# Stick-breaking attention: two heads' values become one 128-column stationary, their transposed weights move as 256 columns in three fp32r products, and the buffer pools change from 17 and 5 to 16 and 7

## The chip, the core and the metric

The kernel runs on one core of one Trainium2 chip, as one program. The metric is device time in microseconds (us), from the runs listed below. The engines are named as the profile names them: PE is the matmul engine and PEld its weight loads, DVE the vector engine, ACT the scalar engine, POOL the engine that starts gathers and scatters, SP the queue that starts the weight loads from HBM.

## The reference

The program is a two-layer trunk over 512 tokens of width 1024. Layer 0 mixes tokens with a state-space mixer and a pooling mixer. Layer 1 mixes them with stick-breaking attention. Each layer then has a mixture of 16 experts. Only the attention is touched by the change:

```python
# 16 heads x 64, strictly causal, swept in 128-query blocks
for blk in range(s // SB_BLOCK):
    q0 = blk * SB_BLOCK
    end = q0 + SB_BLOCK
    z = jnp.einsum('bhqd,bhkd->bhqk', q[:, :, q0:end], k[:, :, :end]) * scale
    causal = s_pos[None, :] < t_pos[:, None]
    log_keep = jnp.where(causal, jax.nn.log_sigmoid(-z), 0.0)
    log_after = lax.cumsum(log_keep, axis=3, reverse=True) - log_keep
    wts = jnp.where(causal, jnp.exp(jax.nn.log_sigmoid(z) + log_after), 0.0)
    outs.append(jnp.einsum('bhqk,bhkd->bhqd', wts, v[:, :, :end]))
```

## The kernel before

**Products.** Most products are in float32 split in two parts: `split` (L81 to L83) writes a high part with ACT and a low part (source minus high) with DVE, both of type fp32r. `mm3` (L85 to L89) then makes three products: stationary high with moving high (L87), stationary high with moving low (L88), stationary low with moving high (L89). A few products are made in plain float32. In the trace each plain float32 matmul stands as two records and each fp32r matmul as one.

**Attention.** `mixer1` (L615 to L717) projects values (`vproj`, 96 products), queries (`query`) and keys (`key`, 48 products each) and runs eight calls of `attend(g, o)`, each for two heads. The program's order is v0, q0, k0, A00, q1, A01, k1, A10, v1, q2, A11, k2, A20, q3, A21, k3, A30, A31, out projection; A20 is `attend(2, 0)`. An attend runs over four query blocks `qb`, with n = 128, 256, 384 and 512 keys. For both heads `s` of a block: scores into a bank of tag B (L672 to L674), two sigmoids on ACT (L676, L677), a running product on DVE (the scan, L679), a product on DVE (L680); then 128x128 transposes into a bank of tag T (L686), a copy back to SBUF (L687, on ACT or DVE, whichever the planner finds free), and the products with the values (L691) in plain float32. In L691 the two heads have 64 stationary columns each, and write to the two halves of one bank `po`, which is kept for the whole attend and split into the output `cat` at its end (L693). L664 writes one element of `po` at the start of the attend.

**Buffers.** Slots of tag raw hold 8 KB for each partition (`NR` = 17 of them): the streamed weights, and every large tile (inputs, transposed inputs, values, queries, keys, outputs). Buffers of tag h hold 4 KB (`NH` = 5). PSUM has four banks of tag A (projections, `po`, the out projection, which needs all four at once, L728), two of B and two of T.

**What sets the order.** The kernel is written in the program's order above, and a planner in the framework puts each engine's instructions in an order of their own: of the instructions that are ready it takes the earliest of the program. So a projection fills PE while an attend that stands before it in the program waits for ACT and DVE. Buffers of one tag are handed out in the order in which the program first writes them: a bank of tag A cannot be taken by a projection before the `po` that stands ahead of it in the program has been written once. Each engine then works through its own list in order, and waits for the others by semaphores. `weights` (L109) splits a streamed weight into a ring of buffers (tags wh, wl) and first asks for the loads that lie one (attention) or six (experts) ahead.

The lines that the prediction's steps touch:

```python
            po = self.bank("A", "pA")            # L663
            v.memset(po[:, 0:1], 0.0)            # L664
...
                kw = [self.half4("kw"), self.half4("kw")]          # L668
...
                    nc.any.tensor_copy(kp[:, :n], pT[:, :n])       # L687
...
            self.split(cat[hh][:, pg * 2 + o], cat[2 + hh][:, pg * 2 + o], po)   # L693
...
        ps = [self.bank("A", "pA") for _ in range(NT)]             # L728
```

Of the kernel before, what the change touches and what calls it, by code (L numbers as in the profile page):

```python
# [8 lines left out]
F32R = mybir.dt.float32r  # L9
BF = mybir.dt.bfloat16  # L10
I32 = mybir.dt.int32
AF = mybir.ActivationFunctionType
# [5 lines left out]
NT = 4  # L18
# [2 lines left out]
EPS = 1e-5  # L21
NE = 16
CAP = 96
NR = 17
RING = 6
NH = 5
GATES = (-1, -1, 7, 15)
OVER = 12
NEG = -1e30
# [9 lines left out]
class Trunk:  # L39
# [18 lines left out]
    def slot(self, name, dt=F32):  # L58
        return self.sb.tile([128, 2048], dt, tag="raw", bufs=NR, name=name)

    def half4(self, name, dt=F32):
        return self.sb.tile([128, 1024], dt, tag="h", bufs=NH, name=name)

# [551 lines left out]
    def mixer1(self):  # L615
        nc, v = self.nc, self.nc.vector
        X = self.xt_pair("x2T")
        for i in range(NT):
            self.transposes(self.xt[i], i, X)
        cat = [None] * 4  # L620
        st = [{}, {}]

        def vproj(hh):
            w = self.weights(1) + self.weights(1)
            vs = self.slot(f"v{hh}").rearrange("p (i d) -> p i d", i=NT)
            for i in range(NT):
                p = self.bank("A", "pA")
                self.proj_x(p, i, X, w)
                nc.scalar.activation(vs[:, i], p, AF.Copy)
            return vs  # L630

        def heads():
            w = self.weights(1)
            for o in range(2):
                p = self.bank("A", "pA")
                for kb in range(KB):
                    os = slice(o * 128, (o + 1) * 128)
                    self.mm3(p, (w[kb][0][:, os], w[kb][1][:, os]), self.op(X, kb), kb == 0, kb == KB - 1)
                for s in range(2):
                    yield 2 * o + s, p, slice(s * 64, s * 64 + 64), slice(64 - s * 64, 128 - s * 64)  # L640

        def query():
            Q = self.half("Q", "S")
            for h, p, r, q in heads():
                nc.scalar.activation(Q[r, h], p[r], AF.Copy)
                v.tensor_tensor(Q[q, h], p[r], Q[r, h].bitcast(F32), op=OP.subtract)
            return Q

        def key():
            H, L = self.half("K", "H"), self.half("K", "L")  # L650
            for h, p, r, q in heads():
                nc.scalar.activation(H[r, h], p[r], AF.Copy)
                v.tensor_tensor(L[r, h], p[r], H[r, h].bitcast(F32), op=OP.subtract)
                v.tensor_copy(H[q, h], H[r, h].bitcast(F32))
                v.tensor_copy(L[q, h], L[r, h].bitcast(F32))
            return H, L

        def attend(g, o):
            hh, pg = g // 2, g % 2
            Q, (H, L), vs = qs_[g], ks_[g], vs_[hh]  # L660
            if pg == 0 and o == 0:
                cat[hh], cat[2 + hh] = self.half("o", f"h{hh}"), self.half("o", f"l{hh}")
            po = self.bank("A", "pA")  # L663
            v.memset(po[:, 0:1], 0.0)  # L664
            for qb in range(NT):
                n = (qb + 1) * 128
                qs = slice(qb * 128, n)
                kw = [self.half4("kw"), self.half4("kw")]  # L668
                for s in range(2):
                    h = 2 * o + s  # L670
                    pS = self.bank("B", "pB")
                    nc.tensor.matmul(pS[:, :n], Q[:, h, qs], H[:, h, :n], start=True, stop=False)  # L672
                    nc.tensor.matmul(pS[:, :n], Q[:, h, qs], L[:, h, :n], start=False, stop=False)
                    nc.tensor.matmul(pS[:, qs], self.identb, self.tri, start=False, stop=True)  # L674
                    kp, sg = kw[s][:, :512], kw[s][:, 512:]
                    nc.scalar.activation(kp[:, :n], pS[:, :n], AF.Sigmoid, scale=-0.125)  # L676
                    nc.scalar.activation(sg[:, :n], pS[:, :n], AF.Sigmoid, scale=0.125)  # L677
                    rv = kp[:, :n][:, ::-1]
                    v.tensor_tensor_scan(rv, rv, rv, 1.0, op0=OP.mult, op1=OP.min)  # L679
                    v.tensor_tensor(sg[:, :n - 1], sg[:, :n - 1], kp[:, 1:n], op=OP.mult)  # L680
                for s in range(2):
                    kp, sg = kw[s][:, :512], kw[s][:, 512:]
                    pT = self.bank("T", "pT")
                    for kb in range(qb + 1):
                        ks = slice(kb * 128, (kb + 1) * 128)
                        nc.tensor.transpose(pT[:, ks], sg[:, ks], self.ident)  # L686
                    nc.any.tensor_copy(kp[:, :n], pT[:, :n])  # L687
                for kb in range(qb + 1):
                    for s in range(2):
                        hc = (pg * 4 + 2 * o + s) * 64  # L690
                        nc.tensor.matmul(po[s * 64:s * 64 + 64, qs], vs[:, kb, hc:hc + 64],  # L691
                                         kw[s][:, kb * 128:(kb + 1) * 128], start=(kb == 0), stop=(kb == qb))
            self.split(cat[hh][:, pg * 2 + o], cat[2 + hh][:, pg * 2 + o], po)  # L693

        vs_, qs_, ks_ = [vproj(0)], [query()], [key()]
        attend(0, 0)
        qs_.append(query())
        attend(0, 1)
        ks_.append(key())
        attend(1, 0)  # L700
        vs_.append(vproj(1))
        qs_.append(query())
        attend(1, 1)
        ks_.append(key())
        attend(2, 0)
        qs_.append(query())
        attend(2, 1)
        ks_.append(key())
        attend(3, 0)
        attend(3, 1)  # L710
        if "att" in self.dbgs:
            for a in range(2):
                t = self.slot(f"dbg{a}")
                v.tensor_tensor(t.rearrange("p (k t) -> p k t", k=4), cat[a].bitcast(F32), cat[2 + a].bitcast(F32), op=OP.add)
                nc.sync.dma_start(self.dbgs["att"][:, a], t.rearrange("p (k t) -> p k t", k=4))
        for _ in self.out_proj(cat, 1, (0, 1)):
            pass  # L717
# [592 lines left out]
```

## Time and profile before

| | |
|---|---|
| runs | 1233.97, 1232.09 and 1228.96 us |
| median | 1232.09 us |
| the profiled execution's own time | 1232.32 us |
| its span, first to last instruction | 1230.7 us |
| mean granted PE clock | 0.985 |
| PE, DVE, ACT busy | 94%, 78%, 61% |
| the eight attends, first scores to the last output split | 608.7 to 797.4 us |
| the experts of layer 1 | about 890 to 1190 us |

A busy PE is one with a matmul in its pipeline, so 94% does not mean that the array worked at its peak for that share. The distance from one matmul's start to the next matmul's start tells what one costs in a dense run.

### The profile page before, as it was taken

To read this page: it belongs to the slowest core of one execution; us is meant where nothing else is said; L and a number is where in the kernel's file an instruction comes from. 1 tells how busy PE (TensorE), PEld (TensorE's weight loads), DVE (VectorE), ACT (ScalarE), POOL (GpSimd) and SP (SyncE) were. 2 spreads that over 40 slices of the span, in tenths; PEclk is the share of its full clock that TensorE was granted. 3 is DMA by queue.
4 is the path that set the end of the run, shared out by engine and by line. 5 is a ranking of instruction groups with operands and counts; after the bars stand their busy time and mean duration, and the time that the engine had idled before them with its cause. 6 is when DMAs were issued, how large, how long until landed. Compare 5 with 4: busy or idle time off the path is not lost. (4 is left out here: it accounts for less than half of the span.)

```text
span 1230.7 us, 17431 instructions
## 1 busy us (share of the span) xinstructions
PE 1162.8 (94%) x6479; PEld 888.6 (72%) x6479; DVE 959.1 (78%) x1381; ACT 750.9 (61%) x1063; POOL 134.9 (11%) x150
## 2 busy tenths in 40 slices
PE   6967999999999999999999999999999999999995
PEld 4856779777768776777777767688877767777674
DVE  6997866798986998785576467755799896989786
ACT  4322542688876888763465456523488885888761
POOL 5010020111010101100000000011101100011101
PEclk9998999999999999999999999998999999999998
DMA  8225662599996998972121024434299998899971
GB/s 254 69 78 184 223 232 97 183 372 377 379 377 247 357 388 325 355 283 69 35 76 63 1 69 153 150 145 163 61 361 387 385 378 304 287 397 356 305 276 70
DMA packets 158166, 285.13 MB, mean 232 GB/s; under 512 B 19584, under 2 KB 43664, under 8 KB 157008
## 3 DMA queue, kind: packets, MB, share of 16 engines
q1 hardware_dynamic: 143760, 256.56, 58.5%
q0 software_dynamic: 9568, 25.19, 6.0%
q10 hardware_dynamic: 4736, 2.10, 0.6%
q8 instruction: 55, 0.90, 0.3%
q14 instruction: 47, 0.39, 0.1%
HBM read 272.02 MB, written 20.19 MB: 237 GB/s over the span
## 5 line engine op out<-in xcount | busy, mean ns | idle before, releaser
L83 DVE TENSOR_TENSOR w_0l<-raw,w_0h 128x1024 fp32r<-128x1024 f32 (+1 forms) x233 | 280.0, 1202 | 53.7 <-ACT w_0h L82 49.4
L82 ACT ACTIVATE w_0h<-raw 128x1024 fp32r<-128x1024 f32 (+1 forms) x233 | 242.5, 1041 | 41.2 <-PE pA L89 22.2
L83 DVE TENSOR_TENSOR w_2l<-raw,w_2h 128x1024 fp32r<-128x1024 f32 x205 | 249.8, 1218 | 15.9 <-ACT w_2h L82 15.5
L82 ACT ACTIVATE w_2h<-raw 128x1024 fp32r<-128x1024 f32 x205 | 216.6, 1057 | 49.7 <-PE pA L89 40.3
L87 PE MATMUL pA<-w_0h,g 128*96 128x512 f32 x256 | 104.2, 407 | 0.8 <-ACT g L82 0.7
L88 PE MATMUL pA<-w_0l,g 128*96 128x512 f32 x256 | 101.2, 395 | 1.8 <-DVE w_0l L83 1.8
L89 PE MATMUL pA<-w_0h,g 128*96 128x512 f32 x256 | 101.5, 397 | 0.3 <-DVE g L83 0.3
L89 PE MATMUL pA<-w_2h,g 128*96 128x512 f32 x256 | 101.5, 397 | 0.0
L87 PE MATMUL pA<-w_2h,g 128*96 128x512 f32 x256 | 101.1, 395 | 0.0
L88 PE MATMUL pA<-w_2l,g 128*96 128x512 f32 x256 | 100.3, 392 | 0.0
L979 POOL DMA_INDIRECT yd<-ysb,ixm x30 | 37.7, 1256 | 441.9 <-ACT ysb L1052 421.4
L89 PEld LDWEIGHTS pA<-w_0h,g 128*96 128x96 f32 x256 | 41.3, 161 | 18.8 <-DVE g L83 2.1
L88 PEld LDWEIGHTS pA<-w_2l,g 128*96 128x96 f32 x256 | 41.5, 162 | 17.9
L89 PEld LDWEIGHTS pA<-w_2h,g 128*96 128x96 f32 x256 | 41.3, 161 | 18.0
L87 PEld LDWEIGHTS pA<-w_2h,g 128*96 128x96 f32 x256 | 41.3, 161 | 17.7
L88 PEld LDWEIGHTS pA<-w_0l,g 128*96 128x96 f32 x256 | 41.6, 163 | 17.2 <-DVE w_0l L83 3.8
L973 POOL DMA_INDIRECT xg<-xd,ixm x32 | 37.4, 1170 | 149.0 <-PE pT L995 79.1
L87 PEld LDWEIGHTS pA<-w_0h,g 128*96 128x96 f32 x256 | 41.5, 162 | 15.7 <-ACT g L82 3.1
L87 PE MATMUL pB<-w_0h,sT 128*96 128x512 f32 x128 | 50.7, 396 | 1.2 <-ACT sT L82 1.2
L679 DVE TENSOR_TENSOR_SCAN kw<-kw 128x128 f32<-128x128 f32 (+3 forms) x64 | 50.2, 813 | 0.9 <-ACT kw L676 0.6
L88 PE MATMUL pB<-w_0l,sT 128*96 128x512 f32 x128 | 50.5, 394 | 0.4 <-DVE w_0l L83 0.4
L89 PE MATMUL pB<-w_0h,sT 128*96 128x512 f32 x128 | 50.8, 397 | 0.0
(442 smaller groups left out, 2810.9 us busy)
## 6 DMA issues: line engine op xcount, KB each, us to landing
raw<-in_moe_w_dram SPq DMA_DIRECT2D x192, 1024.0 KB, 10.1
raw<-in_sb_w_qkv_dram SPq DMA_DIRECT2D x12, 1024.0 KB, 5.1
raw<-in_ple_w_gate_dram SPq DMA_DIRECT2D x8, 1024.0 KB, 8.4
yt<-yd SPq DMA_DIRECT2D x8, 1024.0 KB, 8.1
raw<-in_ab_w_out_dram SPq DMA_DIRECT2D x4, 1024.0 KB, 6.4
xd<-x0r POOLq DMA_DIRECT2D x8, 512.0 KB, 4.1
raw<-in_sb_w_out_dram SPq DMA_DIRECT2D x4, 1024.0 KB, 5.6
raw<-in_ab_w_in_dram SPq DMA_DIRECT2D x3, 1024.0 KB, 7.7
```

The costliest lines, as they stand in the source:

```text
L82: return (self.nc.scalar.activation(hi, src, AF.Copy), (self.nc.gpsimd if pool else self.nc.vector).tensor_tensor(lo, src, hi.bitcast(F32) ...
L83: (self.nc.gpsimd if pool else self.nc.vector).tensor_tensor(lo, src, hi.bitcast(F32), op=OP.subtract))
L87: t.matmul(out, s[0], m[0], start=first, stop=False)
L88: t.matmul(out, s[0], m[1], start=False, stop=False)
L89: t.matmul(out, s[1], m[0], start=False, stop=last)
L679: v.tensor_tensor_scan(rv, rv, rv, 1.0, op0=OP.mult, op1=OP.min)
L973: return nc.gpsimd.indirect_dma_start(out=xgs[:CAP, e % 2, :], out_offset=None, in_=xd[:, :], in_offset=bass.IndirectOffsetOnAxis(ap=self. ...
L979: nc.gpsimd.indirect_dma_start(out=yd[:, :], out_offset=bass.IndirectOffsetOnAxis(ap=self.iy[:CAP, e:e + 1], axis=0), in_=src[:CAP], in_of ...
```

## The change

The values of a pair of heads are now split into a high and a low part (two slots instead of one for each of the two value tiles). The four sub-buffers of a query block, kp and sg for both heads, are laid out by kind, and the transposed weights go to new buffers, wTh and wTl, split as well: the copy L687 becomes a `split`, so the copy is ACT's and DVE gets a subtraction for each. The products with the values become `mm3` with 128 stationary columns (two heads) and 256 moving columns (both heads' weights); of each result one half belongs to a head with itself and is used, the other half crosses the heads and is not. One bank now holds two query blocks, so an attend takes two banks of tag A, the first at its block 0 and the second at its block 2, and each is split by four instructions on half the partitions. The memset of L664 goes. There are 16 slots of 8 KB instead of 17 and 7 of 4 KB instead of 5.

```diff
-NR = 17
+NR = 16
-NH = 5
+NH = 7
...
         def vproj(hh):
             w = self.weights(1) + self.weights(1)
-            vs = self.slot(f"v{hh}").rearrange("p (i d) -> p i d", i=NT)
+            vh, vl = (self.slot(f"v{hh}{a}", F32R).rearrange("p (i d) -> p i d", i=NT) for a in "hl")
             for i in range(NT):
                 p = self.bank("A", "pA")
                 self.proj_x(p, i, X, w)
-                nc.scalar.activation(vs[:, i], p, AF.Copy)
-            return vs
+                self.split(vh[:, i], vl[:, i], p)
+            return vh, vl
...
-            po = self.bank("A", "pA")
-            v.memset(po[:, 0:1], 0.0)
+            hc = (pg * 4 + 2 * o) * 64
+            po = None
             for qb in range(NT):
...
-                kw = [self.half4("kw"), self.half4("kw")]
+                kps, sgs = (self.half4(x).rearrange("p (s k) -> p s k", s=2) for x in ("kp", "sg"))
...
+                wh, wl = (self.half4(x, F32R).rearrange("p (s k) -> p s k", s=2) for x in ("wTh", "wTl"))
                 for s in range(2):
...
-                        nc.tensor.transpose(pT[:, ks], sg[:, ks], self.ident)
-                    nc.any.tensor_copy(kp[:, :n], pT[:, :n])
+                        nc.tensor.transpose(pT[:, ks], sgs[:, s, ks], self.ident)
+                    self.split(wh[:, s, :n], wl[:, s, :n], pT[:, :n])
+                if qb % 2 == 0:
+                    po = self.bank("A", "pA")
                 for kb in range(qb + 1):
+                    ks = slice(kb * 128, (kb + 1) * 128)
+                    self.mm3(po[:, (qb % 2) * 256:(qb % 2) * 256 + 256],
+                             tuple(x[:, kb, hc:hc + 128] for x in vs), (wh[:, :, ks], wl[:, :, ks]), kb == 0, kb == qb)
+                if qb % 2:
+                    pv = po.rearrange("p (q s t) -> p q s t", q=2, s=2)
                     for s in range(2):
-                        hc = (pg * 4 + 2 * o + s) * 64
-                        nc.tensor.matmul(po[s * 64:s * 64 + 64, qs], vs[:, kb, hc:hc + 64],
-                                         kw[s][:, kb * 128:(kb + 1) * 128], start=(kb == 0), stop=(kb == qb))
-            self.split(cat[hh][:, pg * 2 + o], cat[2 + hh][:, pg * 2 + o], po)
+                        r = slice(s * 64, s * 64 + 64)
+                        ts = slice((qb - 1) * 128, n)
+                        hi, lo = (c[r, pg * 2 + o, ts].rearrange("p (q t) -> p q t", q=2)
+                                  for c in (cat[hh], cat[2 + hh]))
+                        self.split(hi, lo, pv[r, :, s])
```

## Rows read from the trace of the kernel before

**Rows 1.** The page: the span, and busy time of each engine.

```profile
span 1230.7 us, 17431 instructions
PE 1162.8 (94%) x6479; PEld 888.6 (72%) x6479; DVE 959.1 (78%) x1381; ACT 750.9 (61%) x1063; POOL 134.9 (11%) x150
```

**Rows 2.** Stretches (attends A00, A21, A30, A31, all): busy PE, PEld, DVE, ACT, POOL, clock, DMA.

```profile
608.70:624.90 16.20, 15.10 (x104) 10.33 (x103) 12.15 (x22) 10.08 (x27) 0.00 (x0) 1.00 0.00 1
...
737.10:761.00 23.90, 23.82 (x140) 17.21 (x140) 18.40 (x29) 15.28 (x32) 0.00 (x0) 1.00 0.26 91
761.00:784.90 23.90, 22.72 (x143) 16.61 (x143) 21.38 (x41) 15.43 (x39) 1.12 (x2) 1.00 0.61 199
784.90:797.40 12.50, 12.39 (x82) 7.97 (x82) 8.73 (x14) 7.08 (x18) 1.81 (x1) 1.00 0.50 170
608.70:797.40 188.70, 183.67 (x1089) 133.74 (x1088) 132.81 (x224) 107.44 (x242) 2.93 (x3) 1.00 0.25 82
```

**Rows 3.** Busy time by stretch: A00's scores and chain, then the projection behind it.

```profile
609.40:624.60 15.20, 14.10 (x98) 9.54 (x97) 12.15 (x22) 9.77 (x26) 0.00 (x0) 1.00 0.00 1
626.50:631.70 5.20, 5.20 (x24) 4.31 (x23) 3.34 (x4) 3.20 (x4) 0.00 (x0) 1.00 0.00 0
```

**Rows 4.** One group, 560 to 802 us: count, busy us, mean ns, idle us before.

```profile
L691 PE MATMUL pA<-kw,v 128*64 128x128 f32 x320 | 33.2, 286 | 0.6 <-DVE kw L687 0.3
```

**Rows 5.** PE in order of time, A30 into A31 (start us, duration us).

```profile
783.61 1.09 PE L691 MATMUL pA<-kw,v 128*64 128x128 f32 x14
784.63 0.33 PE L686 MATMUL pT<-ident,kw 128*128 128x128 f32 x1
...
786.34 0.39 PE L88 MATMUL pA<-w_2l,oh 128*128 128x512 f32 x1
786.57 0.40 PE L89 MATMUL pA<-w_2h,ol 128*128 128x512 f32 x1
786.89 0.43 PE L691 MATMUL pA<-kw,v 128*64 128x128 f32 x2
787.26 0.44 PE L672 MATMUL pB<-KH,QS 128*128 128x384 f32 x1
```

**Rows 6.** PE in order of time in a gate projection: the first of 24 products, and the one behind them.

```profile
1033.29 0.28 PE L87 MATMUL pG<-w_0h,oh 128*128 128x256 f32 x1
...
1036.16 0.28 PE L87 MATMUL pG<-w_0h,oh 128*128 128x256 f32 x1
```

**Rows 7.** Groups by shape: DVE and ACT instructions that read a PSUM bank.

```profile
L83 DVE TENSOR_TENSOR ol<-pA,oh 128x512 fp32r<-128x512 f32 x8 | 5.5, 690 | 16.8 <-ACT oh L82 16.7
...
L687 DVE COPY kw<-pT 128x256 f32<-128x256 f32 x7 | 2.9, 419 | 0.1
...
L687 DVE COPY kw<-pT 128x128 f32<-128x128 f32 x1 | 0.3, 292 | 0.3 <-PE pT L686 0.3
...
L83 DVE TENSOR_TENSOR g<-pT,g 128x384 fp32r<-128x384 f32 x64 | 32.7, 550 | 11.6 <-ACT g L82 11.5
...
L687 ACT COPY kw<-pT 128x256 f32<-128x256 f32 x9 | 3.4, 394 | 0.0
```

**Rows 8.** One line and one tile: L664; then tag A's products from 764 to 798 us.

```profile
L664 DVE MEMSET pA<- x8: 59/59/59, 601.8 to 764.5; 128x1 f32 x8
...
L691 PE MATMUL pA<-kw,v x80: 272/273/324, 773.2 to 797.1; 128*64 128x128 f32 x80
...
L87 PE MATMUL pA<-w_0h,oh x6: 391/436/497, 767.0 to 795.4; 128*128 128x512 f32 x6
```

**Rows 9.** Busy time by stretch: layer 0's mixer, and two of layer 1's experts.

```profile
90.00:100.00 10.00, 0.08 (x1) 0.11 (x1) 9.66 (x15) 0.00 (x0) 0.00 (x0) 0.54 0.67 188
...
970.00:990.00 20.00, 20.00 (x96) 14.22 (x95) 18.05 (x19) 16.96 (x21) 2.47 (x2) 1.00 1.04 389
...
1010.00:1030.00 20.00, 18.95 (x88) 12.84 (x87) 16.63 (x18) 15.40 (x19) 2.42 (x2) 1.00 1.04 381
```

More of the change, by code (lines that the diff above doesn't have):

```diff
@@ L674, in attend @@
                     nc.tensor.matmul(pS[:, qs], self.identb, self.tri, start=False, stop=True)
-                    kp, sg = kw[s][:, :512], kw[s][:, 512:]
+                    kp, sg = kps[:, s], sgs[:, s]
                     nc.scalar.activation(kp[:, :n], pS[:, :n], AF.Sigmoid, scale=-0.125)
@@ L680, in attend @@
                     v.tensor_tensor(sg[:, :n - 1], sg[:, :n - 1], kp[:, 1:n], op=OP.mult)
+                wh, wl = (self.half4(x, F32R).rearrange("p (s k) -> p s k", s=2) for x in ("wTh", "wTl"))
                 for s in range(2):
-                    kp, sg = kw[s][:, :512], kw[s][:, 512:]
                     pT = self.bank("T", "pT")
```

## The prediction

> **What bounds the kernel now.** I read the page first, for the span and the engines [rows 1]: PE is busy 94% of 1230.7 us, DVE 78%. Then the table by stretch, to see what holds inside the attention [rows 2]. From the first scores to the last output the eight attends take 188.7 us, with PE busy 183.67, DVE 132.81, ACT 107.44. The reader is to see two things there: PE hardly rests, and DVE is the next engine, closer in the attends (21.38 of 23.9 us in A30) than its mean shows. A finer table cuts A00 from what comes behind it [rows 3]: in the attend's 15.2 us PE is busy 14.10 and DVE 12.15; then come 5.2 us in which PE runs 24 projection products and nothing else, DVE 3.34. So a projection fills PE's gaps during an attend, and its second half runs alone. One such product costs 5.20 / 24 = 0.217 us.
>
> From that I split PE's 183.7 us. The stretch holds six query or key projections of 48 products, v1 with 96, and 33 products of the out projection (the row of six products is one of six such groups [rows 8]): 417 x 0.217 = 90.5 us. The attends themselves are the other 93 us, 11.7 each. An attend with a 48-product projection is 11.7 + 10.4 = 22.1 us of PE, against 23.9 us taken by A21's stretch [rows 2]: PE sets the pace with some 1.8 us of loss.
>
> **The value products on PE.** Before: 320 records, busy 33.2 us [rows 4]. In a dense run 14 records take 784.63 - 783.61 = 1.02 us, 73 ns each; a visit of two takes 0.37 us, and the product ahead of that visit 0.32 us where its like took 0.23 [rows 5], so entering costs some 0.09. After: 8 attends x 10 key blocks x 3 products = 240, of a shape that the trace has, 128x256 fp32r with 128 stationary columns: 24 of them take 1036.16 - 1033.29 = 2.87 us, 0.120 each [rows 6], 28.7 us in all, up to 31.6 if each of the 32 query blocks still pays 0.09. The saving is at most 33.2 + 2.9 - 28.7 = 7.4 us; if all of before had gone at 73 ns (23.3 us) it would be a loss of 5 to 8. I take -4 us, near the measured busy time, 0.5 for each attend.
>
> The Trainium skill speaks for the change twice. "FP8 and Floating Point Precision", TensorE Precision Notes, gives true FP32 four passes: two heads would be 4 x 2 x 128 = 1024 columns for a key block, against 3 x 256 = 768, and 33.2 us would become 24.9, 8 us less. The trace differs in dense runs: a key block's four records cost 0.29 us there, the new three products 0.36, since the two heads' matmuls overlap. "TensorEngine Tiling (Array Packing)", Key Properties, says that a change of the tiling mode drains TensorE; by that rule the 64-column matmuls pay at each visit, and the 0.32 against 0.23 agrees.
>
> **DVE.** Added: 64 subtractions that read a transpose bank, 16 of each size. By the rows of the same operation or of a copy from the same bank they cost 0.292, 0.419, 0.550 and 0.690 us [rows 7]: 16 x 1.951 = 31.2 us. Gone: DVE's copies of L687, 2.9 + 0.3 = 3.2. The output splits: 32 of 64 partitions by 256 columns instead of 8 of 128 by 512. The trace has no such shape from PSUM; between 0.292 (half the columns) and 0.690 (twice) I take 0.419, the row with 256 columns: 13.4 - 5.5 = 7.9 (3.8 to 16.6). The memset of 8 x 0.059 goes [rows 8]. The values' low parts: 8 x 0.690, half of them (v1) in the stretch, 2.8, hidden under the projection that makes them. Sum in the stretch: 31.2 - 3.2 + 7.9 - 0.5 + 2.8 = 38.2, from 132.8 to 171.0 us of 188.7; for one attend 35.4 / 8 = 4.4 us.
>
> ACT gets DVE's eight copies (3.2) and, for 8 large output copies, 32 small ones at 0.394 [rows 7], 12.6: at most 107.4 + 15.8 = 123 of 188.7 us, hidden by its idle time; it costs only where a chain waits for it (below).
>
> **The chain.** An attend's work on DVE grows from A00's 12.15 us to 16.6, and the scans, products and subtractions hang on each other through ACT and PE. So a chain of about 16.6 us now paces an attend whose own PE work is 11.2 us.
>
> **What fills PE.** Here the removed memset matters. L664 gave `po` its bank at the attend's start, so that the projection that follows in the program could take the next banks at once. The trace shows how early: the last memset is at 764.5, the first out product at 767.0, while the two last attends' value products run from 773.2 to 797.1 [rows 8]. After, the first write of the second `po` is block 2's first value product. Blocks 0 to 2 are (128 + 256 + 384) / 1280 = 60% of an attend: 10 us of chain, in which PE has 6.7 us of its own, then nothing. It rests 3.3 us. After that the projection's 10.4 us and the attend's other 4.5 us are more than the chain's last 6.6, so PE paces again. An attend with its projection becomes 10 + 14.9 = 24.9 us of pace for 22.1, +2.8 us; six of them (A00 to A21), +16.8.
>
> A30 and A31 have only the out projection to fill with, whose four banks come behind A31's second `po`. Before they took 23.9 + 12.5 = 36.4 us [rows 2]. After: k3's second half (5.2 us, as q1's [rows 3]), two chains 33.2, and of the 33 out products (7.2 us) what A31's last block does not cover: its 6.6 us of chain less 4.5 of PE leave room for 2.1, so 5.1 remain. Together 43.5, +7.1.
>
> **Buffers.** 16 slots, of which the values take two more: three fewer for streams during the attention. DMA is at a share of 0.25 there [rows 2]; a load that has to wait for an attend's keys could cost one transfer, 1 MB at 389 GB/s [rows 9] = 2.7 us, at three keys: 0 to 8, I take 0. In the experts PE is busy 20.00 of 20 us with loads at a share of 1.04; in another stretch PE gets only 18.95 [rows 9], so loads just keep up. One megabyte less in hand costs 0 to 2.7 us for each layer; I take 1 for both. The two more 4 KB buffers: four are used for a block where two were, so they buy nothing in the attention; elsewhere I count nothing, as PE is full there.
>
> **Sum.** 16.8 + 7.1 + 1 = +25 us (PE's saving is inside the first two). The profiled execution took 1232.3 us, 0.2 over the median: 1257 us.
>
> **Rivals.**
> *PE stays the bound, and the saving arrives.* It is the other side: -4 us (to -7.4), 1228 (1225 to 1231). It needs DVE to do 171.0 us of work in 185, 92%. For it: DVE does 18.05 of 20 in the experts [rows 9]. Against: there nothing chains it, and in the attention only A30 comes to 89% [rows 2]. It decides if PE rests less than half a microsecond more in an attend than before. By the rule of four passes above (the Trainium skill, "FP8 and Floating Point Precision") the saving would be 8.3 us and the time 1224.
> *The barred fill does no harm.* If DVE's chain alone sets the pace, DVE's idle 3.05 us in A00's stretch [rows 3] takes up part of the 4.4: +1.4 an attend, +11, with the buffers 1244 (1238 to 1250).
> *The chain gets gaps.* Tag h is handed out in order too: a block's kp cannot be written before the block ahead has first written its wTl, so ACT's sigmoid stands in DVE's way once a block. At 0.394 us [rows 7], 32 blocks, that is +13: 1270 (1264 to 1278).
> *The clock falls.* Where PE was idle 9.92 of 10 us the granted clock was 0.54 [rows 9], so part of that stretch ran at 1.2 GHz, not 2.4. If an attend's rests did that, its first 6.7 us of PE would take 13.4, 3.4 more than the chain: +27 on top, 1284. Against: the rests here are a microsecond or so at a time.
> *Nothing to be seen*: terms cancel within 6 us.
>
> **How the numbers follow.** A measurement of this kernel can tell about 0.5%, 6 us. Forecast (1250 to 1264) 0.48; PE stays bound 0.14; harmless bar 0.16; gaps 0.12; clock 0.05; nothing 0.05. Faster than 1226: half of the second, 0.07. Within 0.5%: the rest of it, "nothing", and a little of the third, 0.15. Slower: 0.78. The range leaves out most of the faster rival (0.12), the clock (0.05) and the top of the gaps (0.03): 1230 to 1276. The forecast's own range is 1250 to 1264, from the bounds of the output splits and of PE's saving.
>
> **What would show it.** Right: in the attention stretch PE's busy share falls to some 85 to 90% with DVE at 80% or more; no projection product between an attend's first scores and its block 2's value products; out products start only after A31's block 2; 240 value products 0.12 us apart in runs; ACT and DVE with 64 splits of transposes; the experts as long as before within 5 us. Wrong: PE at 97% in the stretch, or projection products spread through whole attends (then the bank's order does not bind), or the experts longer by 10 us (then the slot was the cost).

## The result and the profile after

The changed kernel took 1293.63 us (median of 4 runs, 1290.90 to 1296.11), the kernel before 1232.96 us beside it (4 runs): a ratio of 1.0498, 95% interval 1.0465 to 1.0531, or +60.7 us. The forecast was 1257, its range ended at 1276: the direction was right, the size was not, and the time lies beyond even the slowest rival (1284).

The page of the changed kernel answers to [rows 1]. PE is busy for 27 us more, although it has fewer products; DVE has 42 us more, ACT 9.

```profile
span 1291.1 us, 17346 instructions
PE 1189.9 (92%) x6399; PEld 917.4 (71%) x6399; DVE 1001.2 (78%) x1461; ACT 759.8 (59%) x1095; POOL 135.3 (10%) x150
```

The table by stretch of the changed kernel (columns as in [rows 2]: busy time of PE, PEld, DVE, ACT, POOL, then granted clock, DMA's share and GB/s): A00 from its first scores to its block 2's first value product, from there to A01's first scores, the same for A01 to A10, and the eight attends with the last output split.

```profile
610.00:625.50 15.50, 10.72 (x47) 8.15 (x45) 12.19 (x25) 8.11 (x24) 0.00 (x0) 0.67 0.00 0
625.50:641.00 15.50, 14.92 (x78) 12.27 (x79) 10.66 (x15) 7.45 (x12) 0.00 (x0) 1.00 0.01 1
641.00:655.00 14.00, 11.04 (x47) 7.63 (x45) 11.51 (x22) 8.43 (x24) 0.00 (x0) 0.63 0.12 26
655.00:670.20 15.20, 14.73 (x77) 12.12 (x78) 8.79 (x16) 5.02 (x10) 0.00 (x0) 1.00 0.32 115
...
610.00:855.50 245.50, 207.54 (x998) 162.38 (x997) 172.32 (x302) 117.55 (x274) 2.93 (x3) 0.86 0.17 55
```

The stretch grew from 189.8 us (cut in the same way, 608.9 to 798.7) to 245.5: +55.7 of the 60.4 us between the two spans. The rest is about 1 us ahead of it and 3.6 behind it. Each attend now has two halves, where before the projection's products filled PE's gaps in the attend [rows 3]. In the first PE does the attend's own 47 records, rests a fifth to a third of the time, and is granted 0.67 or 0.63 of its clock; in the second it is full, at clock 1.00, with the projection's products. A mean clock of 0.86 over 245.5 us is 0.14 / 0.5 x 245.5 = 69 us at 1.2 GHz, where before there was none [rows 2].

The border between the halves is the one that the prediction named. PE's timeline at A00's block 2, and at A31's:

```profile
625.46 0.39 PE L87 MATMUL pA<-wTh,v0h 128*128 128x256 f32 x1 [0.63 <-ACT wTh L82]
625.68 0.39 PE L87 MATMUL pA<-x2Th,w_0h 128*128 128x512 f32 x1
...
845.84 0.38 PE L87 MATMUL pA<-wTh,v1h 128*128 128x256 f32 x1 [0.64 <-ACT wTh L82]
846.07 0.40 PE L87 MATMUL pA<-w_0h,oh 128*128 128x512 f32 x1
```

The first projection product starts 0.2 to 0.3 us after the first write of the second `po`, in every one of the six attends from A00 to A21, and the out products start behind A31's, at 846.1 where before they started at 767.0 [rows 8]. So the barred fill is there. What is new is the length of the first half: 14.6 us as a mean over these six (11.9 to 17.1), where the prediction had 10. In the kernel before, A00 was at its block 2 after 10.1 us (608.9 to 619.0).

The main cause of that is seen in ACT's timeline. The changed kernel's A00, from its first sigmoid:

```profile
610.65 0.26 ACT L676 ACTIVATE kp<-pB 128x128 f32<-128x128 f32 x1
...
615.17 0.28 ACT L82 ACTIVATE wTh<-pT 128x128 fp32r<-128x128 f32 x1 [3.08 <-PE pT L686]
615.34 0.38 ACT L676 ACTIVATE kp<-pB 128x256 f32<-128x256 f32 x1
615.82 0.28 ACT L82 ACTIVATE wTh<-pT 128x128 fp32r<-128x128 f32 x1
...
618.52 0.38 ACT L82 ACTIVATE wTh<-pT 128x256 fp32r<-128x256 f32 x1 [1.59 <-PE pT L686]
618.80 0.49 ACT L676 ACTIVATE kp<-pB 128x384 f32<-128x384 f32 x1
```

ACT stands for 3.08 us at the split of block 0's transposes. The sigmoids of block 1, whose scores PE had finished about three us before, stand behind that split in ACT's list and start 0.17 us after it; block 2's stand in the same way behind block 1's. The table of waits says the same of the whole stretch (us in total, times, longest): ACT waited 51.7 us at wTh for transposes, and 20.6 us at the copy L687 in the kernel before. First before, then after:

```profile
ACT kw L687 <- PE pT L686: 20.6, 21, 2.4
ACT wTh L82 <- PE pT L686: 51.7, 37, 3.2
```

### The profile page after: what moved, and what is told of

Its sections match the earlier page's. It is cut to its first block, busy times and chain, and to the rows that moved or that the text cites. A ratio compares the mean times of both kernels' runs of the same rounds, so it can differ in the third digit from the quotient of the medians.

```text
span 1291.1 us, 17346 instructions
## 1 busy us (share of the span) xinstructions
PE 1189.9 (92%) x6399; PEld 917.4 (71%) x6399; DVE 1001.2 (78%) x1461; ACT 759.8 (59%) x1095; POOL 135.3 (10%) x150
## 5 line engine op out<-in xcount | busy, mean ns | idle before, releaser
L82 ACT ACTIVATE wTh<-pT 128x128 fp32r<-128x128 f32 (+3 forms) x64 | 27.5, 438 | 53.7 <-PE pT L686 51.7
L679 DVE TENSOR_TENSOR_SCAN kp<-kp 128x128 f32<-128x128 f32 (+3 forms) x64 | 51.7, 818 | 0.5
L87 PE MATMUL pB<-w_0h,sT 128*96 128x512 f32 x128 | 50.7, 396 | 1.2 <-ACT sT L82 1.2
L686 PE MATMUL pT<-ident,sg 128*128 128x128 f32 x160 | 36.3, 341 | 16.6 <-DVE sg L680 16.5
```

Of the source, the lines that this page charges most:

```text
L82: return (self.nc.scalar.activation(hi, src, AF.Copy), (self.nc.gpsimd if pool else self.nc.vector).tensor_tensor(lo, src, hi.bitcast(F32) ...
L87: t.matmul(out, s[0], m[0], start=first, stop=False)
L686: nc.tensor.transpose(pT[:, ks], sgs[:, s, ks], self.ident)
```

## The experiments

Two theories stood against each other at first. *Bar*: the projections may not start before block 2, so PE rests, its clock falls, and the rest follows. *Chain*: DVE's 31 us of subtractions lengthen each attend whatever fills PE. Two more came from the trace: *tag order* (a block's kp comes behind the wTl of the block ahead, since both are of tag h) and *clock* (1.2 GHz in the first halves). All times below are medians, and the differences are against the kernel before run beside them on the same chip.

| run | us | ratio to before, 95% interval | difference |
|---|---|---|---|
| e1_claim | 1253.62 | 1.0164 (1.0147 to 1.0181) | +20.0 |
| e2_before_two_banks | 1258.44 | 1.0194 (1.0170 to 1.0218) | +24.8 |
| e3_fill | 1320.93 | 1.0707 (1.0690 to 1.0725) | +87.3 |
| e4_tags | 1272.45 | 1.0327 (1.0302 to 1.0351) | +38.8 |
| e5_claim_tags | 1243.83 | 1.0097 (1.0077 to 1.0117) | +10.3 |
| e6_no_low | 1250.42 | 1.0141 (1.0121 to 1.0162) | +16.9 |
| e7_before_slots | 1239.25 | 1.0056 (1.0040 to 1.0072) | +5.7 |
| e8_fill_light | 1300.40 | 1.0549 (1.0525 to 1.0574) | +66.9 |
| e9_more_buffers | 1307.48 | 1.0606 (1.0584 to 1.0628) | +75.3 |
| e10_after_no_low | 1289.07 | 1.0465 (1.0443 to 1.0487) | +56.9 |
| e11_before_nr18 | 1234.90 | 1.0018 (1.0009 to 1.0028) | +2.7 |
| e12_two_claimed | 1235.51 | 1.0029 (1.0020 to 1.0038) | +3.3 |
| e13_fill_late | 1298.70 | 1.0544 (1.0519 to 1.0568) | +66.1 |

**e1_claim: the bar undone.**

```diff
-            po = None
+            pos = [self.bank("A", "pA") for _ in range(2)]
+            for p in pos:
+                v.memset(p[:, 0:1], 0.0)
...
-                if qb % 2 == 0:
-                    po = self.bank("A", "pA")
+                po = pos[qb // 2]
```

> The changed kernel with both banks of an attend claimed by a one-element memset at the attend's start, and nothing else changed. If the barred fill (with the lower clock that follows PE's rests) is the loss: projection products run from the attend's first scores on, the granted clock stays at 1.0, and the attention stretch falls from 245 to 190 to 205 us, the kernel to 1236 to 1253. If DVE's longer chain sets the pace whatever fills PE: the stretch stays above 230 us, 1275 to 1295. If tag h's order sets it: above 1270.

40.7 of the 60.7 us came back. The stretch in its table:

```profile
613.60:821.20 207.60, 189.77 (x1023) 145.48 (x1021) 171.27 (x316) 117.78 (x275) 2.93 (x3) 0.98 0.19 65
```

It is 38 us shorter than the changed kernel's, with the clock back at 0.98. DVE's busy time is the same 171 us, so DVE can do that work in 208 us or less: its sum was not the bound of 245. But 1253.6 lies just over the top of what *bar* alone allowed: something is left.

**e2_before_two_banks: the bar alone, in the kernel before.**

```diff
-            po = self.bank("A", "pA")
-            v.memset(po[:, 0:1], 0.0)
+            po = None
...
+                if qb % 2 == 0:
+                    po = self.bank("A", "pA")
...
-                        nc.tensor.matmul(po[s * 64:s * 64 + 64, qs], vs[:, kb, hc:hc + 64],
+                        nc.tensor.matmul(po[s * 64:s * 64 + 64, (qb % 2) * 128:(qb % 2) * 128 + 128], vs[:, kb, hc:hc + 64],
...
-            self.split(cat[hh][:, pg * 2 + o], cat[2 + hh][:, pg * 2 + o], po)
+                if qb % 2:
+                    ts = slice((qb - 1) * 128, n)
+                    self.split(cat[hh][:, pg * 2 + o, ts], cat[2 + hh][:, pg * 2 + o, ts], po[:, :256])
```

> The kernel before with only the bank part of the change: no memset, and blocks 0 and 1 in one bank, blocks 2 and 3 in a second, products and values as before in plain float32. If the barred fill is the loss, it shows without any of the new work: projection products start 0.2 us after an attend's block 2 products, and the time rises by 25 to 45 us, to 1257 to 1278, with the clock at half speed in the attends' first parts. If the new work on DVE is the loss: 1228 to 1238.

+24.8 us, without one subtraction of the new work, at the lower edge of what *bar* asked for. A00's first half, its second, and the whole stretch of the profiled execution, which is the longest of the four (1264.0 us):

```profile
608.70:618.40 9.70, 7.70 (x48) 4.98 (x47) 8.75 (x18) 7.32 (x21) 0.00 (x0) 1.00 0.00 0
618.40:634.60 16.20, 15.63 (x92) 11.72 (x90) 9.13 (x12) 7.55 (x12) 0.00 (x0) 1.00 0.20 66
608.70:824.50 215.80, 198.60 (x1071) 142.97 (x1070) 132.74 (x220) 110.99 (x256) 3.10 (x3) 0.92 0.21 71
```

9.7 + 16.2 us is nearly the 10 + 14.9 that the prediction gave a barred attend, here at clock 1.00 and with the old DVE work. So the bar is a loss by itself, of about the size of the whole forecast, and the old chain is as long as what the prediction took for the new one. Two things limit this. The attend's second bank itself is a part of the 24.8 us, 3.3 of them by e12_two_claimed below. And later first halves did fall to 1.2 GHz, as the expectation had it (0.92 over the stretch).

**e4_tags: the order of tag h undone, the banks left barred.**

```diff
-        return self.sb.tile([128, 1024], dt, tag="h", bufs=NH, name=name)
+        return self.sb.tile([128, 1024], dt, tag="w" if name[0] == "w" else "h", bufs=2 if name[0] == "w" else NH - 2, name=name)
```

> The changed kernel with wTh and wTl in a tag of their own (two buffers) and five left in tag h, so that a block's kp need not come after the wTl of the block ahead. If the order of tag h is what stretches the chain: 13 us or more back, 1265 to 1281. If the bar and the clock are the loss: within 6 us of the changed kernel, 1288 to 1300.

21.9 us came back, more than *tag order* asked for. ACT's timeline in A00:

```profile
610.82 0.26 ACT L676 ACTIVATE kp<-pB 128x128 f32<-128x128 f32 x1
...
612.29 0.38 ACT L676 ACTIVATE kp<-pB 128x256 f32<-128x256 f32 x1
...
613.78 0.99 ACT L676 ACTIVATE kp<-pB 128x384 f32<-128x384 f32 x2 [0.29 <-PE pB L674]
615.14 0.28 ACT L82 ACTIVATE wTh<-pT 128x128 fp32r<-128x128 f32 x1 [0.37 <-PE pT L686]
```

The sigmoids of blocks 1 and 2 now stand ahead of block 0's split and start 1.5 and 3.0 us after the first, where in the changed kernel they started 4.7 and 8.2 us after it. A00 is at its block 2 after 12.5 us, for 15.5 in the changed kernel and 10.1 in the one before: the order of tag h is 3.0 of the 5.4 us in it. The next attend moves forward too: A01's first two scores start at 619.8 and 621.9, ahead of A00's block 2 (622.6), where in the changed kernel A01 starts at 641.0.

**e9_more_buffers: number or order of the buffers.**

```diff
-RING = 6
-NH = 7
+RING = 5
+NH = 9
```

> The changed kernel with nine buffers in tag h instead of seven (the weights' ring gives up one pair for them). e4_tags gave back 21 us with no more buffers in all. If it is the order in which one tag is handed out, and not the number of buffers, that holds a block's kp behind the wTl ahead: the attention stretch stays at 240 to 250 us. If seven buffers were too few: the stretch falls to 225 or less, as in e4_tags (222).

The stretch stays as long, and ACT's list is as in the changed kernel, with nine buffers:

```profile
614.40:857.10 242.70, 202.41 (x998) 157.50 (x997) 170.31 (x301) 116.69 (x273) 2.92 (x3) 0.90 0.17 55
```

```profile
615.05 0.26 ACT L676 ACTIVATE kp<-pB 128x128 f32<-128x128 f32 x1
...
619.58 0.28 ACT L82 ACTIVATE wTh<-pT 128x128 fp32r<-128x128 f32 x1 [3.09 <-PE pT L686]
619.75 0.38 ACT L676 ACTIVATE kp<-pB 128x256 f32<-128x256 f32 x1
```

So it is the order of one tag, not how many buffers it has. The kernel as a whole is 14 us slower than the changed one, ahead of the stretch (it starts 4.4 us later) and behind it (448 us to the end for 436). The pair that the weights' ring gave up may be the reason; no run here shows it.

**e5_claim_tags: both orders undone together** (the diffs of e1_claim and e4_tags).

> Both undone together: the banks claimed at the attend's start as in e1_claim (-40 us there) and wTh and wTl in a tag of their own as in e4_tags (-21 us there); the value products and their splits stay. If the bar and tag h's order are two separate losses that add up, the new work itself costs nothing: 1230 to 1240. If they overlap (either alone lets the other part hide): 1244 to 1254, and what is left is the longer chain of DVE, which then is busy 20 us or more of each attend's 23.7. If PE's 4 us come through: 1226 to 1232.

1243.8, at the lower edge of what overlapping allowed. The two edits give back 40.7 and 21.9 us alone and 50.4 together, so 12 us are common to both. A likely reading is that what the order of tag h adds to the first half costs more when that half has no fill. Read in sequence, the order of tag h costs 21.9 us under the bar, and the bar 28.5 without it. 10.3 us are left. The stretch, and one attend of it (A20's first scores to A21's):

```profile
611.60:809.40 197.80, 185.12 (x1014) 144.55 (x1013) 167.36 (x316) 118.75 (x274) 2.94 (x3) 0.98 0.20 68
...
725.60:749.50 23.90, 22.26 (x124) 16.60 (x123) 20.98 (x40) 14.61 (x34) 0.00 (x0) 1.00 0.05 18
```

DVE is busy 21 of 23.9 us, as expected of a longer chain of DVE; the next two runs ask whether that is what holds the attend up. PE's busy time of 185.1 us is what the kernel before has in its stretch, 184.8. The saving on the value products does not show. I summed the distance from each value product's start to the next start on PE, from the first scores to k3's last product (six attends): 240 records take 24.2 us before, 180 take 24.2 us here, 0.403 us for each key block of two heads either way.

**e6_no_low and e10_after_no_low: DVE's subtractions left out**, from e5_claim_tags and from the changed kernel. In both the low part of the weights is left out of the result, and PE keeps 240 products; in e10 a copy of one column still writes to wTl first. e6's diff against e5:

```diff
-                    self.split(wh[:, s, :n], wl[:, s, :n], pT[:, :n])
+                    nc.scalar.activation(wh[:, s, :n], pT[:, :n], AF.Copy)
...
-                    self.mm3(po[:, (qb % 2) * 256:(qb % 2) * 256 + 256],
-                             tuple(x[:, kb, hc:hc + 128] for x in vs), (wh[:, :, ks], wl[:, :, ks]), kb == 0, kb == qb)
+                    pq = po[:, (qb % 2) * 256:(qb % 2) * 256 + 256]
+                    nc.tensor.matmul(pq, vs[0][:, kb, hc:hc + 128], wh[:, :, ks], start=(kb == 0), stop=False)
+                    nc.tensor.matmul(pq, vs[1][:, kb, hc:hc + 128], wh[:, :, ks], start=False, stop=False)
+                    nc.tensor.matmul(pq, vs[0][:, kb, hc:hc + 128], wh[:, :, ks], start=False, stop=(kb == qb))
```

> As e5_claim_tags without the 64 subtractions that write wTl; the middle product takes wTh instead, so PE has the same 240 products and the low part of the weights is left out of the result. If DVE's added work is what is left of the loss: 1224 to 1234, the same as before or a little faster, with PE at 97% in the stretch. If it is the slots, the halves of banks or the copies on ACT: within 6 us of e5_claim_tags.

> The changed kernel without the 64 subtractions that write wTl (the middle product takes wTh, and the low part of the weights is left out of the result); a copy of one column still writes to wTl first, so that tag h is handed out in the same order, and the banks stay barred. If DVE's 31 us of new work are what lengthens the chain ahead of block 2, as the prediction had it: 25 us or more back, under 1270. If it is the orders of banks and of tag h, with DVE waiting inside them: less than 12 us back, 1282 to 1296.

With the orders undone, leaving the subtractions out gains nothing: e6_no_low's stretch has 24 us less on DVE and is 1.9 us longer than e5_claim_tags', and the kernel takes 6.6 us more. With the orders in place it gains 9.5 us in the stretch and 3.8 in the kernel; A00 is at its block 2 after 14.1 us, for 15.5. First e6_no_low, then e10_after_no_low:

```profile
610.10:809.80 199.70, 183.40 (x1002) 143.46 (x1001) 143.04 (x252) 118.31 (x274) 2.92 (x3) 0.97 0.20 67
```

```profile
610.70:846.70 236.00, 194.65 (x992) 153.39 (x991) 151.95 (x302) 116.98 (x274) 2.92 (x3) 0.91 0.17 57
```

So *chain* does not hold as the prediction had it: DVE's added work is worth 0 to 10 us in the stretch, not 25. Both kernels lose some of it again behind the attention (from the stretch to the end 442 us for 433, and 441 for 436); why was not followed up.

**e7_before_slots, e12_two_claimed and e11_before_nr18: what is left, in the kernel before.** e7 has `NR = 16` and `NH = 7`; e12 has e2's two banks, both claimed by memsets as in e1; e11 has `NR = 18` and `RING = 5`.

> The kernel before with 16 slots and 7 small buffers, nothing else. By the prediction the slot costs 1 us (0 to 5): 1232 to 1238. If the missing slot holds up a transfer that something waits for in each projection or each layer's experts: 1240 or more.

> The kernel before with two banks for an attend, both claimed at its start, all the old work and 17 slots. If the second bank itself costs (the out projection gets its four banks later, at the end of the attention): 1236 to 1241, which with the 6 us of the slot accounts for all that is left in e5_claim_tags (10 us). If it does not: 1231 to 1236, and 4 us of e5_claim_tags are the new products and splits.

> The kernel before with 18 slots instead of 17, and the weights' ring smaller by one pair. e7_before_slots lost 6 us with 16 slots. If each slot is worth some 5 us because loads start earlier, and the ring's last pair is not needed: 1226 to 1230, faster than both kernels. If 17 slots are enough, or the ring's pair is worth as much: 1231 to 1245.

The missing slot (with two more small buffers) costs 5.7 us, between the two outcomes that were set down for it. The second bank of each attend, with its second output split, costs 3.3 (interval 2.5 to 4.7), a little less than the expectation asked of it. Together they are 9.0 of the 10.3 us left in e5_claim_tags, and the 1.3 between them is within the intervals. How the second bank costs is seen at the end of the attention. The first out product of the kernel with two claimed banks:

```profile
787.92 0.48 PE L87 MATMUL pA<-w_0h,oh 128*128 128x512 f32 x1
```

It started at 767.0 before: the four banks that the out projection needs now stand behind A31's two, and its products no longer fill A30. The stretch itself is 0.8 us longer than before, the rest of the kernel behind it 2.9. In e7's profiled execution, 10 us longer than that of before, the time went in three places: 3.6 us ahead of the attention, 2.3 in the stretch and 4.1 behind it. An 18th slot, paid for with a pair of the weights' ring, gives nothing (e11: 1.0018), so no kernel here beats the one before.

**e3_fill, e8_fill_light and e13_fill_late: the clock.** All three are the changed kernel with extra products, which write to a half of `po` that real products overwrite, so that PE works where it rested.

```diff
+            def fill(bank, blk):
+                for _ in range(10 if blk < 3 else 0):
+                    nc.tensor.matmul(bank[:, 256:], H[:, 0, :128], H[:, 1, :256], start=True, stop=True)
...
+                if qb == 0:
+                    po = self.bank("A", "pA")
+                fill(po, qb)
                 wh, wl = (self.half4(x, F32R).rearrange("p (s k) -> p s k", s=2) for x in ("wTh", "wTl"))
...
+                fill(po, qb)
-                if qb % 2 == 0:
+                if qb == 2:
                     po = self.bank("A", "pA")
```

This is e3; e8 has six at the first place only. e13 claims the first bank at the attend's start and moves them behind the next block's scores:

```diff
+                if qb == 1:
+                    fill(14)
+                    self.mm3(po[:, :256], tuple(x[:, 0, hc:hc + 128] for x in vs), (wh[:, :, :128], wl[:, :, :128]),
+                             True, True)
...
+                if qb == 0:
+                    continue
+                fill((0, 8, 4, 0)[qb])
```

> The changed kernel with 60 extra products of 256 columns in each attend, 20 for each of blocks 0 to 2, written to a half of po that the block's real products overwrite; they use PE's rests and nothing reads them. The projections stay barred. If the clock is a large part of the loss: the granted clock stays near 1.0 in the attends' first parts, these get shorter by about 4 us each although PE has 7 us more to do, and the time falls to 1255 to 1275. If the bar alone costs (PE's lost time, at any clock), or DVE's chain: no gain, 1290 to 1305.

> As e3_fill (which kept the clock up but put 2.4 us of extra products ahead of each block's own) with 18 extra products in an attend instead of 60, six for each of blocks 0 to 2. If the clock is a good part of the loss, its half-speed time in the stretch falls below half of the changed kernel's 68 us and the time with it, to 1270 to 1288. If the clock costs little, because the chain waits for ACT and DVE anyway: 1290 to 1302.

> The changed kernel with 26 extra products of 256 columns in each attend, which stand behind the next block's scores in PE's list (block 0's value products move behind them), so that they fall into rests and put off little: 14 in the first rest, 8 in the second, 4 in the third. The second bank and tag h's order stay as in the changed kernel. If the lower clock is a part of the loss of its own: less than 20 of the 68 us at half speed stay, the attends' first parts get shorter by 1 to 2.5 us each, and the time falls by 8 to 20 us, to 1274 to 1286. If the chain waits for ACT and DVE at either clock: the half-speed time goes as well, and the time stays within 6 us of 1293.6.

e3 could not settle it, and its 1320.9 us lie outside both of its outcomes: the clock rose, but the planner had put the extra products ahead of the next block's scores (in A00 these came 3.0 us after the attend's first, for 1.1), so the chain was put off while it was sped up. e8, with fewer of them, ended where a cheap clock was expected. e13's A00 reaches block 1's scores after 1.1 us, as the changed kernel's does. Its stretch:

```profile
612.20:859.40 247.20, 214.79 (x1205) 173.35 (x1204) 171.98 (x309) 117.86 (x274) 2.92 (x3) 0.98 0.16 54
```

The clock is at 0.98 for 0.86, some 10 us at half speed for 69, and the stretch is 1.7 us longer. The first halves are shorter by 0.5 us on average (84.3 us for 87.5 in the six attends). That is not yet the price of the clock, because the extra products cost something too: A11's first half, at full clock in both kernels, is 12.8 us in e13 and 11.9 in the changed kernel.

The changed kernel itself has the cleaner comparison. Up to block 2's first value product, A11 and A21 have the same instructions in the same order on PE, ACT and DVE. The first half of A11, then that of A21:

```profile
724.82:736.72 11.90, 8.12 (x46) 5.25 (x44) 10.21 (x22) 8.32 (x25) 0.00 (x0) 1.00 0.07 19
783.75:797.13 13.38, 10.14 (x47) 7.26 (x45) 10.65 (x22) 8.50 (x25) 0.00 (x0) 0.74 0.05 6
```

A21 spent 6.8 us at 1.2 GHz and took 1.5 us longer, and it falls behind A11 from the moment at which the clock fell. A20 has one list as well in the changed kernel and in e9_more_buffers: 15.7 us with 10.2 us at 1.2 GHz, 13.9 with 3.4. A01 likewise: 14.0 with 10.2, and 12.8 with 3.4. So in this chain, which waits mostly for ACT and DVE, a microsecond at 1.2 GHz cost 0.18 to 0.26 us. For the 69 us of the stretch that makes some 12 to 18 us, an estimate from these three pairs. It is no term beside the two orders but a part of what they cost, since the rests that they leave are where the clock fell.

## Why the prediction was wrong, by its steps

- **What bounds the kernel** and **DVE**: right. DVE's busy time in the stretch was forecast at 171.0 us; it measures 172.3 in the changed kernel and 171.3 in e1_claim.
- **The value products on PE**: mis-sized. -4 us was forecast, and 0 was found (24.2 us for 24.2). The prediction added a price for entering to the busy time of before, but in the mixture with other work the 64-column products cost 0.403 us for each key block, as much as three products of 256 columns among others. The 0.09 us for entering, which the prediction took to agree with a drain at a change of mode, is not special to these products: in the kernel before a 512-column product also takes 0.32 us (median) ahead of a transpose with 128 stationary columns, and 0.23 ahead of its like. The rule of four passes (the Trainium skill, "FP8 and Floating Point Precision", TensorE Precision Notes), by which 33.2 us would have become 24.9 as an estimate, does not show in this trace either. That estimate counted the two heads' columns one after the other, and in the dense run of [rows 5] their records start in pairs, some 7 ns apart and 0.11 us from pair to pair, so the two heads' columns did not add up there.
- **The chain** is the step that failed. The prediction took the attend's chain for DVE's work, 16.6 us, with the blocks overlapped as before, so that three fifths of it, 10 us, lay ahead of block 2. DVE's busy time is not the chain's length: 3.0 of A00's 12.15 us are the split of k0 (L653 to L655), and the old chain needs the 10 us already (10.1 before, 9.7 in e2). The new one needs 14.6. What lengthens it is for the larger part not DVE's work (e10: at most 10 us over the stretch) but that blocks no longer overlap: a block's sigmoids stand behind the split of the block ahead. In A00, 5.4 us longer than before, undoing that order takes back 3.0 (e4), and leaving out the subtractions 1.4 (e10). The lower clock, a result of PE's rests, is in it as well (1.5 us in A21); these parts are not independent, and the 2.4 us that stay in e4 are not told apart. 4.6 us in six attends are 27.6 of the 36 us that were missed, and A30 and A31 another 6.4.
- **What fills PE**: the mechanism was right: the barred product comes 0.2 us after the first write of the second `po`. The second halves (without A10's, which holds v1 as well) measure 15.5, 15.3, 16.0, 15.3 and 15.3 us for the forecast's 14.9. For A30 and A31 (from behind A21's last value product, 805.6 to 855.5) the forecast was 43.5 us, and they took 49.9. The bar costs 24.8 us in the kernel before (21.5 without the second bank's 3.3) and 28.5 in the changed one without the order of tag h, for 16.8 + 7.1 = 23.9 in the sum. Its size was met, but in part by luck: the chain's length was taken from the wrong cause.
- **Buffers**: "four are used for a block where two were, so they buy nothing" saw the number and not the order, and the slot was mis-sized, 1 us (bound 5.4 in the experts) for 5.7. That an attend holds two banks, and what this does to the out projection even when both are claimed (3.3 us), was no term.
- **The rivals.** *The chain gets gaps* was this very mechanism, with a chance of 0.12 and a wrong price: one sigmoid of 0.394 us for each block, 13 us. What waits is not one sigmoid but the whole front of the next block, which stands behind it: in A00 block 1 starts 3.2 us later than in e4_tags and block 2 5.2 us later. It costs 21.9 us under the bar and 9.7 without (e1 less e5). The rival's 1270 held the bar as well; at the measured prices the two make 50.4 of the 60.7 us. *The clock falls* came true as an event (0.67 in A00's first half), against the argument that rests are a microsecond or so at a time: PE's longest, ahead of block 0's transposes in A00, is 2.63 us. Its price of +27 was too high: by the pairs above the lower clock cost some 12 to 18 us, an estimate, and inside the price of the two orders, not on top. *PE stays the bound* and *harmless bar* are out: e1 gives back 40.7 us.

The sum, as measured: order of tag h 21.9, bar 28.5 (both with the lower clock that comes with them), slot 5.7, second bank 3.3, 1.3 not told apart: 60.7 us. The slot and the second bank were measured in the kernel before.

## What to carry to other kernels

Where buffers of one tag are handed out in the program's order, list for each tag what stands ahead of each next buffer and when that is first written: a buffer that is written late (a transposed result, an accumulator of a later block) holds back everything behind it, and a claim at the start or a tag of its own gave back most of that here. Price such a wait by all that stands behind the waiting instruction in its engine's list, not by that instruction's own duration. A saving on PE is to be priced by start-to-start distances where the product stands in the mixture, for the old shape as for the new. And where a lower clock is suspected, compare two stretches with the same lists at either clock before filling the rests: the filler has a price of its own.

## What was not expected of the hardware

- A microsecond at a granted clock of 1.2 GHz cost only 0.18 to 0.26 us where PE waits for ACT and DVE: 1.5 us for 6.8 of them in A21 against A11, which has the same instructions at full clock. Keeping the clock up with extra products gave nothing back: with 10 of some 69 us left, the kernel took 1298.7 us for 1293.6 (e13, with 208 extra products in PE's rests).
- Two plain float32 matmuls with 64 stationary columns each, on the two halves of a bank, and three fp32r matmuls with 128 stationary and 256 moving columns took the same time for the same result in the mixture with other products: 0.403 us for each key block, 24.2 us in six attends.
- DVE did 167 to 171 us of work in stretches of 198 and 208 us, with scans, products and subtractions that hang on ACT and PE, and leaving 24 us of it out did not shorten the stretch (199.7 us for 197.8).
